# Moving the operands of TensorE's products to chosen offsets modulo 256 bytes in a four-layer decoder trunk

## Chip, cores and metric

One core of a Trainium2 chip. The metric is the device time of one execution in microseconds; lower is better.

## What is computed

The reference is a trunk of four residual layers over 256 tokens of width 1024, in float32: `x = x + mixer(rms_norm(x))`. Layers 0 and 3 use mixer A, layer 1 mixer B, layer 2 mixer C. Each mixer has one input projection, which also emits a gate z, and one output projection.

```python
def mixer_a(h):     # layers 0 and 3
    u, v, z = split(h @ w_in)                 # 3 x 2048 columns
    v = rms_norm(v, v_gain)
    mixed = einsum("gij,bcjgd->bcigd", tril(w_s), v) + b_s
    return (u * mixed * silu(z)) @ w_out
def mixer_b(h):     # layer 1
    q, k, v, z = split(h @ w_in)              # 3 groups x 8 heads x 128, z 1024
    o = softmax-weighted sum over 3 dilated window attentions of normed, rotated q, k
    return (o * silu(z)) @ w_out
def mixer_c(h):     # layer 2
    xc, z = split(h @ w_in)                   # 2 x 2048 columns
    mixed = per-group w_grp @ (causal_mean(xc, window) - xc) * scale
    return (mixed * silu(z)) @ w_out
```

## The kernel before

Every float32 matrix product is made of three products of a high and a low part (float32r). The helper `mm3` (L75) issues them: L77 multiplies the high stationary by the high moving operand, L78 the high stationary by the low moving one, L79 the low stationary by the high moving one. In `nc.tensor.matmul(out, a, b)` the operand `a` is stationary, 128 columns, and `b` is moving, 128, 256 or 512 columns. Each of these products has its own weight load, which the profile shows as PEld. In the names of the profile, `u<-w30h,hTh` is a product into the tile u whose moving operand is w30h and whose stationary one is hTh.

All weights come as one stream of 272 units of 512 KB, in the order of use. SP loads unit after unit into four buffers (wr). ACT makes the high part of a unit (L82) and DVE the low part (L85), into seven buffers each (w..h, w..l). `step` (L163) is called after every few products, runs due tasks (`tick`, L101) and splits units ahead of use. The order of all work on the engines is written out by these generators: a task issues some instructions and yields the number of ticks after which it goes on.

At the start of a layer `norm_task` and `norm_transpose` (L216 to L243) scale x, transpose it on TensorE (fp32, L222), and write the transposed, gained result as hTh (ACT, L226) and hTl (DVE, L229), each 8 x 256 columns. These two tiles, allocated once (L188, L189) and used by all layers, are read through `h_t` (128 columns, as the stationary operand) and `h_all` (256 columns, as the moving operand).

- `proj_tok` (L253): hT is stationary, 512 columns of w are moving. It makes v, z and u of layers 0 and 3, qk and v01 of layer 1, and the first gate (cz3) of layer 2. One call is 48 products. v2p (L708 to L715) is the same with 256 columns of w.
- `proj_feat` (L277): w is stationary, 256 columns of hT are moving. It makes bz of layer 1, and cx and the other cz of layer 2, 96 products in a call. `group` (L799) does the same with cd in place of hT, into cg, 48 products in a call.
- `proj_out` (L291): the gated result (y, yb or cy) is stationary, 512 columns of w are moving, into wo.
- In layer_a, `mix_task` (L401) multiplies wsr (stationary) by v (moving, 256 columns) into mx. In layer_b, `score_task` (L565) multiplies q (stationary) by k (moving, 128 or 256 columns) into s, and `product` (L641) the values v01 and v2 (stationary) by the transposed probabilities pT (moving, 128 or 256) into o.

SBUF tiles of a pool are laid end to end in the order in which their tags are first used, with all buffers of a tag together. Most sizes are whole multiples of 256 bytes. By these sizes w, the y tiles, v, wsr, qk, v01, pT, yb and cy begin 128 bytes past a multiple of 256, hT 64 bytes past one, and cd at a multiple.

The lines that the change touches are quoted here with the functions that hold them.

Of the kernel before, what the change touches and what calls it, by code (L numbers as in the profile page):

```python
# [48 lines left out]
def hybrid_trunk_kernel(ctx, tc, x, wts, norm_gainT, a_v_gain, a_wsT, a_bsT, b_gl, b_gv, c_scaleT,  # L49
# [18 lines left out]
    def tiny(n, name, tag="t"):  # L68
        return cp.tile([P, n], F32, tag=f"{tag}{n}", name=name, bufs=8)
# [115 lines left out]
    nc.gpsimd.memset(m05_row, -0.5)  # L185
    m05 = m05_row[:, :4]
    junk = cp.tile([P, HALF + 32], BF16, tag="junk", name="junk")[:, :HALF]
    hTh = cp.tile([P, KT, S], F32R, tag="hTh", name="hTh")  # L188
    hTl = cp.tile([P, KT, S], F32R, tag="hTl", name="hTl")  # L189

    warm = atp("warm")
    for _ in range(WARM):
# [23 lines left out]
    def norm_transpose(layer, t, xs):  # L216

        pts = []
        for n in range(2):
            pt = (trp if n else atp)(f"hp{layer}{t}{n}").rearrange("p (k c) -> p k c", c=P)  # L220
            for k in range(4):
                nc.tensor.transpose(pt[:, k], xs[:, n, k * P:(k + 1) * P], ident)  # L222
            pts.append(pt)
        sl = slice(t * P, (t + 1) * P)
        for k in range(KT):
            nc.scalar.activation(hTh[:, k, sl], pts[k // 4][:, k % 4], AF.Copy, scale=gT[:, layer, k:k + 1])  # L226
            yield k
        for k in range(KT):
            nc.vector.scalar_tensor_tensor(hTl[:, k, sl], pts[k // 4][:, k % 4], gT[:, layer, k:k + 1],  # L229
                                           hTh[:, k, sl].bitcast(F32), op0=ALU.mult, op1=ALU.subtract)  # L230
            yield KT + k
# [12 lines left out]

    def h_t(k, t):
        sl = slice(t * P, (t + 1) * P)
        return hTh[:, k, sl], hTl[:, k, sl]

    def h_all(k):
        return hTh[:, k, :], hTl[:, k, :]  # L250


    def proj_tok(name, skew=None):  # L253
# [94 lines left out]
        return kc, wsT, bsT  # L348

    def layer_a(layer, consts, pl, mid):  # L350
        kc, wsT, bsT = consts

        def tmp(tag, name, bufs):
# [6 lines left out]
        def v_task(n, o):  # L360
            vh, vl = pair(pl, [P, 2, HALF], "v", f"v{layer}{n}", 5)
            v.append((vh, vl))
            vv = [tmp("vv", f"vv{layer}{n}{t}", 2) for t in range(2)]
            for t in range(2):
                nc.scalar.activation(junk, o[t], AF.Square, accum_out=vs[t][:, n:n + 1])  # L365
                nc.vector.tensor_tensor(vv[t], o[t], kc[:, n * HALF:(n + 1) * HALF], op=ALU.mult)  # L366
            yield 1
            for t in range(2):
                hi_of(vh[:, t], vv[t])
            yield 1  # L370
            for t in range(2):
                lo_of(vl[:, t], vv[t], vh[:, t])
            done.add(("v", layer, n))
            if n < 3:
                return

            yield 1
            rs = []
            for t in range(2):
                ms = tiny(1, f"vms{layer}{t}")  # L380
                nc.vector.tensor_reduce(ms, vs[t], axis=mybir.AxisListType.X, op=ALU.add)
                me = tiny(1, f"vme{layer}{t}")
                nc.vector.tensor_scalar(me, ms, 1.0 / 2048.0, EPS, op0=ALU.mult, op1=ALU.add)
                r = tiny(1, f"vr{layer}{t}")
                nc.gpsimd.tensor_tensor(r, me, m05[:, 0:1], op=ALU.pow)
                rs.append(r)
            for t in range(2):
                yield 1
                wh, wl = pair(pl, [P, 8, P], "wsr", f"wsr{layer}{t}", 2)
                nc.scalar.activation(wh, wsT, AF.Copy, scale=rs[t][:, 0:1])  # L390
                yield 1
                nc.vector.scalar_tensor_tensor(wl, wsT, rs[t][:, 0:1], wh.bitcast(F32), op0=ALU.mult,
                                               op1=ALU.subtract)
                wsr.append((wh, wl))
            done.add(("wsr", layer))
            mid()
# [84 lines left out]
                                        cs[:, a, t:t + 1, :].to_broadcast([P, 2 * NG, ROPE]), op=ALU.mult)  # L481

    def layer_b(layer, consts, pl):
        gv, msk, rop = consts
        m0, m1 = msk[:, :NG * P], msk[:, NG * P:]
        yT = []
# [1 line left out]
        prob = {}  # L488

        def qk_task(hp, g, o):  # L490
            qh, ql = pair(pl, [P, 4, S], "qk", f"qk{hp}{g}", 4)
            qk[hp, g] = (qh, ql)
            ssq = [tiny(4, f"qs{hp}{g}{t}") for t in range(2)]
            rq = [tiny(4, f"qr{hp}{g}{t}") for t in range(2)]
            qn = [pl.tile([P, 4, HD], F32, tag="qn", name=f"qn{hp}{g}{t}", bufs=2) for t in range(2)]
# [15 lines left out]
            def rotate(t):  # L511

                ra = pl.tile([P, 4, ROPE], F32, tag="ra", name=f"ra{hp}{g}{t}", bufs=1)
                rb = pl.tile([P, 4, ROPE], F32, tag="rb", name=f"rb{hp}{g}{t}", bufs=1)
                for a in range(2):
                    hs = slice(2 * a, 2 * a + 2)
                    c = rop[:, 0, t, g, a:a + 1, :].to_broadcast([P, 2, ROPE])
                    nc.vector.tensor_tensor(ra[:, hs], qn[t][:, hs, :ROPE], c, op=ALU.mult)  # L518
                    for b in range(2):
                        s0, s1 = b * 16, (1 - b) * 16  # L520
                        c = rop[:, 1, t, g, a:a + 1, s0:s0 + 16].to_broadcast([P, 2, 16])
                        nc.vector.tensor_tensor(rb[:, hs, s0:s0 + 16], qn[t][:, hs, s1:s1 + 16], c, op=ALU.mult)  # L522
                nc.vector.tensor_tensor(qn[t][:, :, :ROPE], ra, rb, op=ALU.add)
# [3 lines left out]
            def transpose(t):  # L527
                pts[t] = trp(f"qt{hp}{g}{t}").rearrange("p (h c) -> p h c", c=P)
                for h in range(4):
                    nc.tensor.transpose(pts[t][:, h], qn[t][:, h], ident)  # L530
                for a in range(2):
                    nc.scalar.activation(qh[:, 2 * a:2 * a + 2, t * P:(t + 1) * P], pts[t][:, 2 * a:2 * a + 2],
                                         AF.Copy, scale=gv[:, 2 * g + a:2 * g + a + 1])

            def low(t):
                for a in range(2):
                    d = (slice(None), slice(2 * a, 2 * a + 2), slice(t * P, (t + 1) * P))
                    nc.vector.scalar_tensor_tensor(ql[d], pts[t][:, 2 * a:2 * a + 2], gv[:, 2 * g + a:2 * g + a + 1],  # L538
                                                   qh[d].bitcast(F32), op0=ALU.mult, op1=ALU.subtract)

            square(0)
            square(1)
# [22 lines left out]
        def score_task(hp, h):  # L565
# [8 lines left out]
            rl = [tiny(1, f"rl{hp}{h}{i}", "td") for i in range(2)]  # L574
            s0 = atp(f"s0{hp}{h}")
            for g in range(NG):
                qh, ql = qk[hp, g]
                mm3(s0[:, g * P:(g + 1) * P], (qh[:, h, :P], ql[:, h, :P]), (qh[:, 2 + h, :P], ql[:, 2 + h, :P]),
                    True, True)
            yield 1  # L580
            s1 = [atp(f"s1{hp}{h}{i}") for i in range(2)]
            for g in range(NG):
                qh, ql = qk[hp, g]
                mm3(s1[g // 2][:, (g % 2) * S:(g % 2 + 1) * S], (qh[:, h, P:], ql[:, h, P:]),
                    (qh[:, 2 + h], ql[:, 2 + h]), True, True)
            nc.vector.tensor_tensor_reduce(f0, s0[:, :NG * P], m0, 1.0, -3.0e38, op0=ALU.add, op1=ALU.max,
                                           accum_out=mx[0])
            nc.vector.tensor_scalar(nb[0], mx[0], -SCALE, None, op0=ALU.mult)
# [110 lines left out]
        for hp in range(NHEAD // 2):  # L699
            for g in range(NG):  # L700
                spawn(qk_task(hp, g, proj_tok(f"qk{hp}{g}", skew=layer if hp == 0 and g == 0 else None)))
                if hp == 0 and g == 0:
                    gate(0)
                    gate(1)
            o = proj_tok(f"v01{hp}")
            vh, vl = pair(pl, [P, 2, HALF], "v01", f"v01{hp}", 1)
            spawn(val_task(hp, o, vh, vl))
            vp = pp(f"v2p{hp}")  # L708
            for j in range(2):
                w = [a.rearrange("p a b -> p (a b)") for a in next_unit()]  # L710
                for kk in range(4):
                    k = 4 * j + kk
                    ws = [a[:, kk * 256:(kk + 1) * 256] for a in w]
                    for t in range(2):
                        mm3(vp[:, t * 256:(t + 1) * 256], h_t(k, t), ws, k == 0 and t == 0, k == KT - 1)  # L715
                    if kk % 2:
                        step(kk // 2)
            v2h, v2l = pair(pl, [P, 2, 256], "v2", f"v2{hp}", 1)
            spawn(val2_task(hp, vp, v2h, v2l))
            spawn(mix_task(hp, (vh, vl, v2h, v2l), szT[:, hp]), LAST_LAG if hp == NHEAD // 2 - 1 else MIX_LAG)  # L720

# [6 lines left out]


    def layer_c(layer, pl):  # L730
        csc = pl.tile([P, 32], F32, name="csc")[:, :16]
        nc.gpsimd.dma_start(csc, c_scaleT)
        rcn = pl.tile([P, 4, PAD], F32, name="rcn")
        nc.gpsimd.dma_start(rcn, rcnt)
# [34 lines left out]
        def pool_task(g, xp):  # L769
# [8 lines left out]
            for i in range(2):  # L778
                cur, lag = xc[i], 1
                while lag < w:  # L780
# [6 lines left out]
                d = pl.tile([P, 2, S], F32, tag="cdd", name=f"cdd{g}{i}", bufs=2)  # L787
                nc.vector.scalar_tensor_tensor(d, cur[:, :, PAD:], 1.0 / w, xc[i][:, :, PAD:], op0=ALU.mult,
                                               op1=ALU.subtract)
                e = pl.tile([P, 2, PAD], F32, tag="ce", name=f"ce{g}{i}", bufs=2)[:, :, :w - 1]  # L790
                nc.vector.tensor_tensor(e, cur[:, :, PAD:PAD + w - 1],
                                        rcn[:, g:g + 1, :w - 1].to_broadcast([P, 2, w - 1]), op=ALU.mult)
                nc.vector.tensor_tensor(d[:, :, :w - 1], e, xc[i][:, :, PAD:PAD + w - 1], op=ALU.subtract)
# [253 lines left out]
```

## Time and profile before

| what | value |
|---|---|
| time, median of 3 runs (lowest to highest) | 847.12 us (846.95 to 847.43) |
| the profiled execution's own time | 846.98 us |
| span of the profile, first to last instruction | 845.3 us |
| TensorE products: busy, count | 834.2 us, 4600 |
| TensorE weight loads: busy, count | 719.2 us, 4600 |
| DVE, ACT, POOL busy | 546.7, 488.6, 56.8 us |
| read from HBM | 147.72 MB |

The profile is of one execution. A product's duration there holds the filling of the array and overlaps with the next product, so the busy share of PE doesn't tell how dense the stream is. The start times do: the distance from the start of one product to the start of the next is what the product adds to the stream. The views of the trace give start times to 0.01 us, so the first and the last row of a stretch, with the number of products between, give the mean distance.

### The profile page before, as it was taken

The page shows a single profiled execution, that of the slowest core. Times are in us where ns is not written, and L with a number is a line of the kernel's source. Part 1 is how long each engine was busy: PE and PEld are TensorE (multiplying, and loading weights), DVE is VectorE, ACT ScalarE, POOL GpSimd, SP SyncE. Part 2 cuts the span into 40 slices and gives each one's busy share as a digit, 9 for nine tenths or more (in the row PEclk, how much of TensorE's full clock was granted, in tenths as well). Part 3 has the DMA queues.
Part 4 walks back from the last instruction along what each step waited for, and adds up shares of the span by engine and source line. Part 5 has one row for each costly group of instructions (what it writes and reads, how often), then busy time and mean ns, then how long its engine had stood idle before and what let it go on. Part 6 is the DMA issues. An engine that isn't in the chain of part 4 may idle for free.

```text
span 845.3 us, 12424 instructions
## 1 busy us (share of the span) xinstructions
PE 834.2 (99%) x4600; PEld 719.2 (85%) x4600; DVE 546.7 (65%) x932; ACT 488.6 (58%) x918; POOL 56.8 (7%) x79
## 2 busy tenths in 40 slices
PE   8999999999999999999999999999999999999998
PEld 6888888888988888888888889999988888888886
DVE  6866556546747667667667576798754786556551
ACT  7665444336768677678678567446543666434340
POOL 1301000001001021021021011000000000000000
PEclk9999999999999999999999999999999999999999
DMA  8756554562755345345345267547664476455541
GB/s 297 268 207 218 197 199 155 180 193 93 253 173 157 119 150 175 124 151 174 125 150 172 79 220 255 176 150 243 203 206 149 140 235 213 158 176 172 174 149 50
DMA packets 41500, 149.57 MB, mean 177 GB/s; under 512 B 4864, under 2 KB 4880, under 8 KB 41184
## 3 DMA queue, kind: packets, MB, share of 16 engines
q1 hardware_dynamic: 40320, 144.72, 51.9%
q0 software_dynamic: 976, 4.05, 1.5%
q8 instruction: 36, 0.59, 0.3%
q14 instruction: 24, 0.20, 0.1%
q10 hardware_dynamic: 144, 0.02, 0.0%
HBM read 147.72 MB, written 1.05 MB: 176 GB/s over the span
## 4 chain that ended last, share of the span: by engine, by line
PE 86%; ACT 7%; DVE 2%; issue 2%; POOL 2%; DMA 1%; SPq 0%; POOLq 0%; DVEq 0%
PE wo L77 6%; PE wo L78 6%; PE wo L79 6%; PE qk L79 4%; PE qk L77 4%; PE qk L78 4%; PE u L79 3%; PE z L79 3%; PE z L77 3%; PE u L77 3%; PE u L78 3%; PE z L78 3%; PE v L79 3%; PE v L77 3%; PE v L78 3%; ACT junk L500 2%
## 5 line engine op out<-in xcount | busy, mean ns | idle before, releaser
L505 POOL TENSOR_TENSOR qr<-qm,m 128x4 f32<-128x4 f32 x24 | 30.3, 1271 | 224.4 <-DVE qm L504 224.4
L509 ACT ACTIVATE qn<-qk,qr 128x128 f32<-128x128 f32 x96 | 27.5, 381 | 15.1 <-POOL qr L505 15.1
L500 ACT ACTIVATE junk<-qk 128x128 bf16<-128x128 f32 x96 | 26.8, 279 | 7.3 <-PE qk L79 4.6
L423 DVE TENSOR_TENSOR sz<-u,sz 128x512 f32<-128x512 f32 x16 | 11.0, 686 | 28.0 <-PE u L79 28.0
L226 ACT ACTIVATE hTh<-hp,gT 128x128 fp32r<-128x128 f32 x64 | 17.5, 382 | 16.1 <-PE hp L222 16.1
L207 POOL TENSOR_TENSOR r<-ms,m 128x1 f32<-128x1 f32 x8 | 5.4, 670 | 285.7 <-DVE ms L205 285.7
L321 DVE TENSOR_TENSOR x<-wo,x 128x512 f32<-128x512 f32 x16 | 11.0, 690 | 20.1 <-PE wo L79 20.0
L229 DVE SCALAR_TENSOR_TENSOR hTl<-hp,gT,hTh 128x128 fp32r<-128x128 f32 x64 | 17.9, 343 | 7.8 <-ACT hTh L226 7.8
L365 ACT ACTIVATE junk<-v 128x512 bf16<-128x512 f32 x16 | 9.6, 600 | 18.1 <-PE v L79 17.9
L500 ACT ACTIVATION_READ_ACCUMULATOR junk<-qk 128x1 f32 x96 | 19.1, 199 | 0.0
L366 DVE TENSOR_TENSOR vv<-v,kc 128x512 f32<-128x512 f32 x16 | 10.9, 689 | 12.7 <-ACT junk L365 12.6
L449 ACT ACTIVATE sz<-z 128x512 f32<-128x512 f32 x16 | 9.4, 597 | 15.5 <-PE z L79 14.9
L518 DVE TENSOR_TENSOR ra<-qn,kcb 128x64 f32<-128x64 f32 x48 | 10.6, 221 | 12.0 <-ACT qn L509 10.9
L530 PE MATMUL qt<-ident,qn 128*128 128x128 f32 x96 | 14.6, 274 | 3.4 <-DVE qk12l L538 0.5
L530 PEld LDWEIGHTS qt<-ident,qn 128*128 128x128 f32 x96 | 11.3, 140 | 7.3 <-issue 2.7
L200 ACT ACTIVATE junk<-x 128x512 bf16<-128x512 f32 x16 | 10.2, 639 | 10.9 <-DVE x L321 9.4
L426 DVE SCALAR_TENSOR_TENSOR yy<-mx,bs,sz 128x256 f32<-128x256 f32 x32 | 14.0, 480 | 0.6
L600 ACT ACTIVATE p<-p,rl 128x384 f32<-128x384 f32 (+1 forms) x16 | 11.5, 769 | 4.8 <-DVE rl L599 4.8
L522 DVE TENSOR_TENSOR rb<-qn,kcb 128x32 f32<-128x32 f32 x96 | 13.8, 184 | 0.0
L596 ACT ACTIVATE p<-p,nb 128x768 f32<-128x768 f32 x8 | 7.5, 938 | 7.9 <-DVE nb L595 7.9
L504 DVE TENSOR_SCALAR qm<-qs 128x4 f32<-128x4 f32 x24 | 3.3, 165 | 12.7 <-ACT junk L500 12.7
L346 POOL TENSOR_SCALAR_AFFINE_SELECT kc<-kc 128x128 f32<-128x128 f32 x16 | 9.2, 612 | 15.4 <-DMA kc<-in_a_wsT_dram 15.4
(2770 smaller groups left out, 3262.0 us busy)
## 6 DMA issues: line engine op xcount, KB each, us to landing
wr<-in_wts_dram SPq DMA_DIRECT2D x272, 512.0 KB, 4.2
kc<-in_a_v_gain_dram POOLq DMA_DIRECT2D x2, 1024.0 KB, 6.1
x<-in_x_dram SPq DMA_DIRECT2D x4, 256.0 KB, 4.9
kc<-in_a_wsT_dram POOLq DMA_DIRECT2D x2, 512.0 KB, 8.8
out_dram<-x SPq DMA_DIRECT2D x4, 256.0 KB, 2.0
kcb<-in_masks_dram POOLq DMA_DIRECT2D x1, 576.0 KB, 8.5
kcb<-in_b_gl_dram POOLq DMA_DIRECT2D x1, 192.0 KB, 6.0
kcb<-in_rope_dram POOLq DMA_DIRECT2D x1, 64.0 KB, 8.4
```

Of the source, the lines that this page charges most:

```text
L77: nc.tensor.matmul(out_ap, lh[0], rh[0], start=start, stop=False, skip_group_check=True)
L78: nc.tensor.matmul(out_ap, lh[0], rh[1], start=False, stop=False, skip_group_check=True)
L79: nc.tensor.matmul(out_ap, lh[1], rh[0], start=False, stop=stop, skip_group_check=True)
L226: nc.scalar.activation(hTh[:, k, sl], pts[k // 4][:, k % 4], AF.Copy, scale=gT[:, layer, k:k + 1])
L229: nc.vector.scalar_tensor_tensor(hTl[:, k, sl], pts[k // 4][:, k % 4], gT[:, layer, k:k + 1], hTh[:, k, sl].bitcast(F32), op0=ALU.mult, op ...
L426: nc.vector.scalar_tensor_tensor(y[:, sl], mxs[n][t][:, sl], bsT[:, 2 * n + gg:2 * n + gg + 1], us[t][:, sl], op0=ALU.add, op1=ALU.mult)
L500: nc.scalar.activation(junk[:, :HD], ov[t][:, h], AF.Square, accum_out=ssq[t][:, h:h + 1])
L505: nc.gpsimd.tensor_tensor(rq[t], ms, m05, op=ALU.pow)
L509: nc.scalar.activation(qn[t][:, h], ov[t][:, h], AF.Copy, scale=rq[t][:, h:h + 1])
L522: nc.vector.tensor_tensor(rb[:, hs, s0:s0 + 16], qn[t][:, hs, s1:s1 + 16], c, op=ALU.mult)
L530: nc.tensor.transpose(pts[t][:, h], qn[t][:, h], ident)
L600: nc.scalar.activation(f, f, AF.Copy, scale=rl[i][:, 0:1])
```

## The change

The change moves tiles in SBUF. hTh and hTl become slices of one tile hT with 64 spare elements; in layer 2 the slices begin at its start, in the other layers 16 elements (64 bytes) later. In layer A a tile st of 16 columns is allocated ahead of wsr, and holds the six small statistics that were in tiny tiles. In layer B the pair of tiles qk has 16 more columns and is split into a part for q, which begins 16 elements later than a multiple of 64, and a part for k, which begins at 0; rb is 16 columns longer; the low part of v2 is 48 columns longer. In layer C csc is 16 columns longer, and ce is 56 columns instead of 32. The number, the shapes and the order of the instructions stay.

```diff
-    hTh = cp.tile([P, KT, S], F32R, tag="hTh", name="hTh")
-    hTl = cp.tile([P, KT, S], F32R, tag="hTl", name="hTl")
+    hT = cp.tile([P, 2 * KT * S + 64], F32R, tag="hT", name="hT")
+
+    def h_parts(layer):
+
+        o = 0 if layer == 2 else 16
+        return [hT[:, o + i * KT * S:o + (i + 1) * KT * S].rearrange("p (k s) -> p k s", s=S) for i in range(2)]
+
+    hcur = [None, None]
...
         sl = slice(t * P, (t + 1) * P)
+        hTh, hTl = h_parts(layer)
         for k in range(KT):
...
     def h_t(k, t):
         sl = slice(t * P, (t + 1) * P)
-        return hTh[:, k, sl], hTl[:, k, sl]
+        return hcur[0][:, k, sl], hcur[1][:, k, sl]

     def h_all(k):
-        return hTh[:, k, :], hTl[:, k, :]
+        return hcur[0][:, k, :], hcur[1][:, k, :]
...
     def layer_a(layer, consts, pl, mid):
+        hcur[:] = h_parts(layer)
         kc, wsT, bsT = consts
...
             rs = []
-            for t in range(2):
-                ms = tiny(1, f"vms{layer}{t}")
+            st = pl.tile([P, 16], F32, name="st")
+            for t in range(2):
+                ms, me, r = (st[:, 8 * t + i:8 * t + i + 1] for i in range(3))
                 nc.vector.tensor_reduce(ms, vs[t], axis=mybir.AxisListType.X, op=ALU.add)
-                me = tiny(1, f"vme{layer}{t}")
                 nc.vector.tensor_scalar(me, ms, 1.0 / 2048.0, EPS, op0=ALU.mult, op1=ALU.add)
-                r = tiny(1, f"vr{layer}{t}")
                 nc.gpsimd.tensor_tensor(r, me, m05[:, 0:1], op=ALU.pow)
...
     def layer_b(layer, consts, pl):
+        hcur[:] = h_parts(layer)
...
         def qk_task(hp, g, o):
-            qh, ql = pair(pl, [P, 4, S], "qk", f"qk{hp}{g}", 4)
-            qk[hp, g] = (qh, ql)
+            parts = pair(pl, [P, 4 * S + 16], "qk", f"qk{hp}{g}", 4)
+
+            qk[hp, g] = [[a[:, o:o + 2 * S].rearrange("p (h s) -> p h s", s=S) for a in parts]
+                         for o in (2 * S + 16, 0)]
...
-                rb = pl.tile([P, 4, ROPE], F32, tag="rb", name=f"rb{hp}{g}{t}", bufs=1)
+                rb = pl.tile([P, 4 * ROPE + 16], F32, tag="rb", name=f"rb{hp}{g}{t}", bufs=1)
+                rb = rb[:, :4 * ROPE].rearrange("p (h c) -> p h c", c=ROPE)
...
             for g in range(NG):
-                qh, ql = qk[hp, g]
-                mm3(s0[:, g * P:(g + 1) * P], (qh[:, h, :P], ql[:, h, :P]), (qh[:, 2 + h, :P], ql[:, 2 + h, :P]),
-                    True, True)
+                qs, ks = qk[hp, g]
+                mm3(s0[:, g * P:(g + 1) * P], [a[:, h, :P] for a in qs], [a[:, h, :P] for a in ks], True, True)
...
-            v2h, v2l = pair(pl, [P, 2, 256], "v2", f"v2{hp}", 1)
+            v2h, v2l = [pl.tile([P, HALF + n], F32R, tag=f"v2{a}", name=f"v2{hp}{a}", bufs=1)[:, :HALF].rearrange(
+                "p (t c) -> p t c", t=2) for a, n in (("h", 0), ("l", 48))]
...
     def layer_c(layer, pl):
-        csc = pl.tile([P, 32], F32, name="csc")[:, :16]
+        hcur[:] = h_parts(layer)
+        csc = pl.tile([P, 48], F32, name="csc")[:, :16]
...
-                e = pl.tile([P, 2, PAD], F32, tag="ce", name=f"ce{g}{i}", bufs=2)[:, :, :w - 1]
+                e = pl.tile([P, 56], F32, tag="ce", name=f"ce{g}{i}", bufs=2)
+                e = e[:, :2 * PAD].rearrange("p (a s) -> p a s", s=PAD)[:, :, :w - 1]
```

## Rows read from the trace of the kernel before

**Rows 1.** The page, busy time of each engine (share of the span) and instructions

```profile
PE 834.2 (99%) x4600; PEld 719.2 (85%) x4600; DVE 546.7 (65%) x932; ACT 488.6 (58%) x918; POOL 56.8 (7%) x79
```

**Rows 2.** The page, TensorE's granted clock in 40 slices of the span, in tenths

```profile
PEclk9999999999999999999999999999999999999999
```

**Rows 3.** The page, the chain that ended last, by engine and by line

```profile
PE 86%; ACT 7%; DVE 2%; issue 2%; POOL 2%; DMA 1%; SPq 0%; POOLq 0%; DVEq 0%
PE wo L77 6%; PE wo L78 6%; PE wo L79 6%; PE qk L79 4%; PE qk L77 4%; PE qk L78 4%; PE u L79 3%; PE z L79 3%; PE z L77 3%; PE u L77 3%; PE u L78 3%; PE z L78 3%; PE v L79 3%; PE v L77 3%; PE v L78 3%; ACT junk L500 2%
```

**Rows 4.** Who waited for whom, TensorE: us in total, times, longest

```profile
PE qt L530 <- DVE qk12l L538: 0.5, 1, 0.5
```

**Rows 5.** Timeline of TensorE, z of layer 3: start us, us, instruction, count

```profile
700.20 0.39 PE L77 MATMUL z<-w224h,hTh 128*128 128x512 f32 x1
...
710.96 0.39 PE L79 MATMUL z<-w227h,hTl 128*128 128x512 f32 x1
```

**Rows 6.** Timeline of TensorE, wo of layer 3, second and last product

```profile
803.13 0.39 PE L78 MATMUL wo<-w258l,y30h 128*128 128x512 f32 x1
...
840.78 0.39 PE L79 MATMUL wo<-w271h,y33l 128*128 128x512 f32 x1
```

**Rows 7.** Timeline of TensorE, layer 1: a stretch of qk, one of wo

```profile
308.37 0.40 PE L78 MATMUL qk<-w98l,hTh 128*128 128x512 f32 x1
...
316.16 0.39 PE L79 MATMUL qk<-w101h,hTl 128*128 128x512 f32 x1
...
488.54 0.40 PE L78 MATMUL wo<-w149l,yb2h 128*128 128x512 f32 x1
...
496.29 0.39 PE L79 MATMUL wo<-w150h,yb3l 128*128 128x512 f32 x1
```

**Rows 8.** Timeline of TensorE, layer 2: one call into cz, one into cg

```profile
561.08 0.28 PE L77 MATMUL cz<-hTh,w174h 128*128 128x256 f32 x1
...
571.88 0.28 PE L79 MATMUL cz<-hTh,w177l 128*128 128x256 f32 x1
571.99 0.28 PE L77 MATMUL cg<-cd2h,w178h 128*128 128x256 f32 x1
...
577.58 0.28 PE L79 MATMUL cg<-cd2h,w179l 128*128 128x256 f32 x1
```

**Rows 9.** Timeline of TensorE: the 12 products of mx00, and 11 of v2p

```profile
72.69 0.28 PE L77 MATMUL mx<-v00h,wsr00h 128*128 128x256 f32 x1
...
73.99 0.28 PE L79 MATMUL mx<-v00h,wsr01l 128*128 128x256 f32 x1
...
267.00 0.28 PE L78 MATMUL v2p<-w88l,hTh 128*128 128x256 f32 x1
...
268.18 0.28 PE L79 MATMUL v2p<-w88h,hTl 128*128 128x256 f32 x1
```

**Rows 10.** Groups of TensorE, the fp32 transposes: busy us, mean ns, idle before

```profile
L434 PE MATMUL yp<-ident,yy 128*128 128x128 f32 x64 | 9.6, 272 | 0.0
L222 PE MATMUL hp<-ident,xs 128*128 128x128 f32 x64 | 8.5, 276 | 0.1
```

**Rows 11.** Instructions of tile wo, two units: duration ns min/median/max, first and last start

```profile
L77 PE MATMUL wo<-w49h,y00h x4: 393/397/476, 155.6 to 157.8; 128*128 128x512 f32 x4
L77 PE MATMUL wo<-w53h,y01h x4: 389/389/389, 167.1 to 169.1; 128*128 128x512 f32 x4
```

**Rows 12.** Timeline of TensorE, layer 1: bz from its second product after a transpose

```profile
219.89 0.28 PE L78 MATMUL bz<-hTl,w71h 128*128 128x256 f32 x1
...
222.48 0.28 PE L79 MATMUL bz<-hTh,w72l 128*128 128x256 f32 x1
```

**Rows 13.** Instructions of tile u, layer 0, one unit: duration ns min/median/max

```profile
L77 PE MATMUL u<-w20h,hTh x4: 394/394/394, 67.2 to 69.3; 128*128 128x512 f32 x4
L78 PE MATMUL u<-w20l,hTh x4: 388/388/388, 67.4 to 69.5; 128*128 128x512 f32 x4
L79 PE MATMUL u<-w20h,hTl x4: 392/392/392, 67.6 to 69.7; 128*128 128x512 f32 x4
```

More of the change, by code (lines that the diff above doesn't have):

```diff
@@ L531, in transpose @@
                 for a in range(2):
-                    nc.scalar.activation(qh[:, 2 * a:2 * a + 2, t * P:(t + 1) * P], pts[t][:, 2 * a:2 * a + 2],
-                                         AF.Copy, scale=gv[:, 2 * g + a:2 * g + a + 1])
+                    nc.scalar.activation(qk[hp, g][a][0][:, :, t * P:(t + 1) * P], pts[t][:, 2 * a:2 * a + 2], AF.Copy, scale=gv[:, 2 * g + a:2 * g + a + 1])
             def low(t):
                 for a in range(2):
-                    d = (slice(None), slice(2 * a, 2 * a + 2), slice(t * P, (t + 1) * P))
-                    nc.vector.scalar_tensor_tensor(ql[d], pts[t][:, 2 * a:2 * a + 2], gv[:, 2 * g + a:2 * g + a + 1],
-                                                   qh[d].bitcast(F32), op0=ALU.mult, op1=ALU.subtract)
+                    qh, ql = (b[:, :, t * P:(t + 1) * P] for b in qk[hp, g][a])
+                    nc.vector.scalar_tensor_tensor(ql, pts[t][:, 2 * a:2 * a + 2], gv[:, 2 * g + a:2 * g + a + 1],
+                                                   qh.bitcast(F32), op0=ALU.mult, op1=ALU.subtract)
             square(0)
@@ L582, in score_task @@
             for g in range(NG):
-                qh, ql = qk[hp, g]
-                mm3(s1[g // 2][:, (g % 2) * S:(g % 2 + 1) * S], (qh[:, h, P:], ql[:, h, P:]),
-                    (qh[:, 2 + h], ql[:, 2 + h]), True, True)
+                qs, ks = qk[hp, g]
+                mm3(s1[g // 2][:, (g % 2) * S:(g % 2 + 1) * S], [a[:, h, P:] for a in qs], [a[:, h] for a in ks],
+                    True, True)
             nc.vector.tensor_tensor_reduce(f0, s0[:, :NG * P], m0, 1.0, -3.0e38, op0=ALU.add, op1=ALU.max,
```

## The prediction

> **What bounds the kernel now.** I read the page's totals first. TensorE's matmul row is busy 834.2 of 845.3 us, while DVE has 546.7 and ACT 488.6 [rows 1]; the granted clock is at nine tenths or more in every slice [rows 2], that is at the 2.4 GHz level, so there is no clock to win. The chain that ended last is 86% PE, and its largest PE lines are the three products of the helper (L77, L78, L79) [rows 3]. The list of who waited for whom gives TensorE almost nothing: seven waits of 0.5 us at a transpose in layer 1, of which one row stands for all [rows 4], and little else. The kernel is a nearly unbroken stream of products, so its time is the sum of the distances between starts of neighbouring products. I therefore work with starts, not with durations, which include the filling of the array and overlap.
>
> Each product has a weight load of its own (the loads are busy 719.2 us beside the 834.2 of the products, so they overlap them [rows 1]), which reads the next stationary operand while the current moving one is still being read. I call "offset" the address of the next product's stationary operand minus that of the current moving one, modulo 256 bytes; it follows from the tile sizes laid end to end in order of first use. Before the change it is 192 for the projections from hT to 512 columns, and 0 for the output projections. With 256 columns it is 64 where w is stationary and hT moving (bz, cz, cx), 128 in cg, 0 in mx and, inside them, in s and o, and 192 in v2p. The kernel before is thus already an experiment on what the change does: the same helper with the same shapes at several offsets.
>
> - 512 columns, offset 192, layer 3: z from its first to its last product is 48 products, 47 distances, (710.96 - 700.20)/47 = 228.9 ns [rows 5].
> - 512 columns, offset 0, layer 3: wo from its second to its last is 166 distances, (840.78 - 803.13)/166 = 226.8 ns [rows 6]. Loops, operand shapes and PSUM use are the same as in z.
> - Layer 1, where other work cuts in: qk at offset 192 has 34 distances, (316.16 - 308.37)/34 = 229.1 ns; wo at offset 0 has 34, (496.29 - 488.54)/34 = 227.9 ns [rows 7].
> - 256 columns, offset 64: cz, 95 distances, (571.88 - 561.08)/95 = 113.7 ns; the same loop at offset 128 in cg, 47 distances, (577.58 - 571.99)/47 = 118.9 ns [rows 8].
> - 256 columns, offset 0: mx, 11 distances, (73.99 - 72.69)/11 = 118.2 ns; offset 192: v2p, 10 distances, (268.18 - 267.00)/10 = 118.0 ns [rows 9].
>
> The rows say that this offset has a price. cz and cg differ in nothing else that I can find: 5.2 ns of 119. These rows speak against a rule of the Trainium skill (TensorE: Matmul & The Clock Gate, "Step-by-step: what each phase is for"): TensorE has two independent read ports, and loading the next weights takes nothing from the running matmul. By that rule all the terms below are zero and the time stays at 847.12 us; that is rival B.
>
> **The change part by part.** No instruction is added or removed: operations, shapes, order and waits stay, only addresses move.
>
> - hT. The new tile is 256 bytes longer than the two it replaces, so everything behind it keeps its place modulo 256. In layers 0, 1 and 3 hT begins 64 bytes later and lies where w lies: offset 192 becomes 0. These are v, z and u of layers 0 and 3 (2 x 3 x 192 = 1152 products) and qk and v of layer 1 (576 + 192 = 768); without those whose successor is another kind, some 1126 and 724 are left. 1126 x (228.9 - 226.8) = 2.4 us, and 724 x (229.1 - 227.9) = 0.9 us: **-3.3 us**. Bounds: 1.2 ns for all 1850 is 2.2 us, 2.1 ns for all is 3.9 us. I keep the two prices apart because layer 1 is interrupted as its wo is. The 48 of layer 2's first cz stay at 192.
> - The side effect on hT as moving operand. bz in layer 1 goes from 64 to 0: 191 x (118.2 - 113.7) = **+0.9 us**. v2p goes from 192 to 0: 180 x (118.2 - 118.0), nothing. For both the nearest row at offset 0 is mx, another product, so bz is bounded by 0 and +1.0 (cg's price) and v2p by -0.8 (offset 64) and +0.2. In layer 2 the tile is taken 64 bytes earlier, so cx and cz stay at 64.
> - csc longer by 64 bytes: cd moves from 0 to 64, cg's offset from 128 to 64: 192 x (118.9 - 113.7) = **-1.0 us**; the longer ce brings cy back to w's place, so that layer's wo stays at 0.
> - st ahead of wsr (64 bytes): mx goes from 0 to 64. The padded rb does it for v01 and v2 (o), the split qk tile for s: q lies 64 past k, except where one group's last product meets the next group's tile. 88 + 68 + 50 products of 256 columns, some 204: 204 x (118.2 - 113.7) = **-0.9 us**. The 116 of 128 columns move the same way; no row shows them at 64. I take 0, since they read half as long, bounded by the 4.5 ns of 256 columns either way, 0.5 us.
> - The fp32 transposes of yy and p move from 0 to 64. They last 272 ns at 0 (yp) and 276 at 128 (hp) [rows 10]: 4 ns for each of 136 at most, half a microsecond, taken as 0.
> - The statistics in st instead of in turning tiny tiles, and hT's one tile for hi and lo: same instructions, same queues, no DMA moved past anything. The writers of hT are 64 pieces of 128 columns as before. Nothing is costed; their cover is the stream of products, and if it were gone an extra wait at a layer's start would cost like the 0.5 us waits [rows 4].
>
> What is late next: a shorter stream brings the transposes of layer 1 earlier to the same DVE work. Seven of them already wait [rows 4]. Between the two transposes of a task lie some 2.5 us of products; they shrink by under 1%, 0.02 us each, 7 x 0.02 = **+0.1 us**. DVE and ACT have 300 us of slack [rows 1].
>
> Sum: -3.3 + 0.9 - 1.0 - 0.9 + 0.1 = -4.2 us. The profiled execution takes 846.98 us (span 845.3), the median of the runs is 847.12, 0.14 more. 846.98 - 4.2 = 842.8, on the median's scale **842.9 us**.
>
> **The rivals.**
>
> A. The forecast: the offset sets the distance, 842.9. For it: cz against cg, z against wo, in the same helper [rows 5, 6, 8].
>
> B. The offset is no cause at 512 columns, or at none. Then 226.8 belongs to something else in wo, and what is left is -1.0 - 0.9 + 0.9 + 0.1 = -0.9, 846.2 us; if it is no cause at all, 847.1. For it: the 512-column difference is under 1% and the two sides are different stages; against it: it is there in layer 3 and again in layer 1 [rows 5 to 7], and the addresses are the only difference that I find. Here belongs also that the tiles don't land where I place them: with hT off by 64 bytes the 512-column term is gone and the time is again about 846.2.
>
> C. Slower: the offset helps only in an undisturbed stream. Some wo products at offset 0 last 397 ns instead of 389 [rows 11], and bz at offset 64 runs at (222.48 - 219.89)/22 = 117.7 ns for 22 distances after it was cut by a transpose, while it had 113.7 before [rows 12]. So there is a second, slower rhythm that the offset alone doesn't exclude. In that rhythm an offset-0 product costs 226.8 + 8 = 234.8, 5.9 more than now. It decides from the point where 2.1/8 = 26% of the 1850 fall into it; at 60% the mean is 231.6, 1850 x 2.7 = +5.0 us; with -0.9 for the rest this gives 851.2 us. Against it: layer 3's wo, 226.8, includes such products already, and layer 1's wo, the most interrupted one, still has 227.9 [rows 6, 7].
>
> **How the numbers follow.** A measurement of this kernel tells 0.2% (1.7 us) from no change. A has 0.86; its own ends are the bounds above: 3.9 + 1.0 + 0.9 with bz free and the unpriced half microseconds in favour, 6.3 us, 840.8; and 2.2 with the unpriced ones against it, about 1.5 to 2 us in all, 845.3. B has 0.10, C 0.04. The range reaches from 840.9 to 845.6: practically all of A, but not B and C (0.14 left out). Faster by over 0.2% is A less 0.01 for its weakest end: 0.85. Within 0.2% are B and that end: 0.11. Slower is C: 0.04.
>
> **What would show it.** In the profile after: z, u, v and qk at about 227 ns from start to start, their durations near 389 ns where they now go round 394, 388, 392 [rows 13]; cg and mx at 113 to 114 ns; bz at 118 or so; wo, cx and later cz as before; the waits of [rows 4] unchanged to 0.1 us. A z that stays at 228.9 makes it B; long stretches of 397 ns make it C. If bz stays at 113.7, only the step on bz is wrong, and the time is 0.9 us lower.

## The result, and the profile after

The change makes the kernel slower: 848.36 us median of 20 runs (847.85 to 848.80) against 846.99 us of 20 runs of the kernel before (846.27 to 847.65). The ratio is 1.0017 with a 95% interval of 1.001 to 1.0024. I had forecast 842.9 us, 4.2 us less; it is 1.4 us more.

The page of the kernel after shows the same picture as [rows 1] to [rows 3]: the same counts, the clock at nine tenths or more, 1 us more of PE.

```profile
span 846.6 us, 12421 instructions
PE 835.2 (99%) x4600; PEld 723.3 (85%) x4600; DVE 546.8 (65%) x932; ACT 488.8 (58%) x918; POOL 57.6 (7%) x79
PE 86%; ACT 7%; DVE 2%; issue 2%; POOL 2%; DMA 1%; SPq 0%; POOLq 0%; DVEq 0%
```

So the answer lies in the distances from start to start. Here is TensorE's timeline of the kernel after (start us, us, instruction, count), first and last row of each stretch, in this order: z and wo of layer 3, bz and v2p of layer 1, cz, cg and cx of layer 2.

```profile
702.29 0.39 PE L77 MATMUL z<-w224h,hT 128*128 128x512 f32 x1
...
712.95 0.39 PE L79 MATMUL z<-w227h,hT 128*128 128x512 f32 x1
...
804.47 0.39 PE L78 MATMUL wo<-w258l,y30h 128*128 128x512 f32 x1
...
842.12 0.39 PE L79 MATMUL wo<-w271h,y33l 128*128 128x512 f32 x1
...
208.78 0.28 PE L77 MATMUL bz<-hT,w68h 128*128 128x256 f32 x1
...
218.73 0.28 PE L79 MATMUL bz<-hT,w71l 128*128 128x256 f32 x1
...
266.89 0.28 PE L78 MATMUL v2p<-w88l,hT 128*128 128x256 f32 x1
...
268.09 0.28 PE L79 MATMUL v2p<-w88h,hT 128*128 128x256 f32 x1
...
562.53 0.28 PE L77 MATMUL cz<-hT,w174h 128*128 128x256 f32 x1
...
573.72 0.28 PE L79 MATMUL cz<-hT,w177l 128*128 128x256 f32 x1
...
573.84 0.28 PE L77 MATMUL cg<-cd2h,w178h 128*128 128x256 f32 x1
...
579.37 0.28 PE L79 MATMUL cg<-cd2h,w179l 128*128 128x256 f32 x1
...
522.96 0.28 PE L77 MATMUL cx<-hT,w160h 128*128 128x256 f32 x1
...
556.76 0.28 PE L79 MATMUL cx<-hT,w171l 128*128 128x256 f32 x1
```

z has 47 distances in 10.66 us, 226.8 ns where it had 228.9 [rows 5]; wo is unchanged, 37.65/166 = 226.8 [rows 6]. bz is now at 9.95/83 = 119.9 ns. The same stretch before, first and last row, had 9.43/83 = 113.6:

```profile
209.78 0.28 PE L77 MATMUL bz<-hTh,w68h 128*128 128x256 f32 x1
...
219.21 0.28 PE L79 MATMUL bz<-hTh,w71l 128*128 128x256 f32 x1
```

v2p is at 1.20/10 = 120 where it had 118.0 [rows 9]. cg came down only to 5.53/47 = 117.7 from 118.9. And cz, whose offset the change leaves at 64, is at 11.19/95 = 117.8 ns where it had 113.7 [rows 8]; the 288 products of cx go the same way, 33.80/287 = 117.8. The view of one tile's instructions (duration ns min/median/max, first and last start) shows it for cx at a glance, first before, then after:

```profile
L77 PE MATMUL cx<-hTh,w160h x8: 276/276/276, 522.7 to 525.1; 128*128 128x256 f32 x8
```

```profile
L77 PE MATMUL cx<-hT,w160h x8: 281/282/282, 523.0 to 525.4; 128*128 128x256 f32 x8
```

The distances of these products, summed by kind over both traces and subtracted, give where the time went. A row can change by up to 0.2 us with the way in which the distances at the seams between kinds are counted:

| products | offset | forecast us | measured us |
|---|---|---|---|
| z, u, v of layers 0, 3 | 192 to 0 | -2.4 | -1.96 |
| qk, v of layer 1 | 192 to 0 | -0.9 | -0.52 |
| bz | 64 to 0 | +0.9 | +1.09 |
| v2p | 192 to 0 | 0 | +0.30 |
| cg | 128 to 64 | -1.0 | -0.19 |
| mx, s, o of 256 columns | 0 to 64 | -0.9 | -0.06 |
| cx | 64, kept | 0 | +1.67 |
| cz of 256 columns | 64, kept | 0 | +1.06 |
| sum | | -4.3 | +1.39 |

All starts of TensorE together, from the first to the last, span 1.34 us more than before, so the kinds that the table leaves out add up to almost nothing; the medians differ by 848.36 - 846.99 = 1.37. The open question was thus why products at an unchanged offset became some 4.4 ns slower. TensorE's timeline at the second pair of transposes of layer 2's first gate gives the hint: before it, cz settles at 113 to 114 ns in both kernels. This is the last transpose and what follows, before:

```profile
515.82 0.27 PE L757 MATMUL czt<-ident,czs 128*128 128x128 f32 x1
515.84 0.37 PE L77 MATMUL cz<-hTh,w157h 128*128 128x256 f32 x1
516.05 0.28 PE L78 MATMUL cz<-hTl,w157h 128*128 128x256 f32 x1
516.17 0.28 PE L79 MATMUL cz<-hTh,w157l 128*128 128x256 f32 x1
516.28 0.28 PE L77 MATMUL cz<-hTh,w157h 128*128 128x256 f32 x1
...
517.19 0.28 PE L79 MATMUL cz<-hTh,w157l 128*128 128x256 f32 x1
```

and after:

```profile
515.78 0.27 PE L768 MATMUL czt<-ident,czs 128*128 128x128 f32 x1
515.81 0.36 PE L77 MATMUL cz<-hT,w157h 128*128 128x256 f32 x1
516.01 0.28 PE L78 MATMUL cz<-hT,w157h 128*128 128x256 f32 x1
516.12 0.28 PE L79 MATMUL cz<-hT,w157l 128*128 128x256 f32 x1
516.24 0.28 PE L77 MATMUL cz<-hT,w157h 128*128 128x256 f32 x1
...
517.18 0.28 PE L79 MATMUL cz<-hT,w157l 128*128 128x256 f32 x1
```

From the fourth product behind the transpose to the last one shown are 8 distances: 0.91 us, 113.8 ns, before; 0.94 us, 117.5 ns, after. Both streams then hold their pace, before to the first cg and after to the last. The products are the same ones at the same offset; something ahead of them decides between two paces.

### The profile page after: what moved, and what is told of

Same layout as the page of the kernel before. It is cut to its first block, busy times and chain, and to the rows that moved or that the text cites. A ratio compares the mean times of both kernels' runs of the same rounds, so it can differ in the third digit from the quotient of the medians.

```text
span 846.6 us, 12421 instructions
## 1 busy us (share of the span) xinstructions
PE 835.2 (99%) x4600; PEld 723.3 (85%) x4600; DVE 546.8 (65%) x932; ACT 488.8 (58%) x918; POOL 57.6 (7%) x79
## 4 chain that ended last, share of the span: by engine, by line
PE 86%; ACT 7%; DVE 2%; issue 2%; POOL 2%; DMA 1%; SPq 0%; POOLq 0%; DVEq 0%
PE wo L77 6%; PE wo L79 6%; PE wo L78 6%; PE qk L77 4%; PE qk L79 4%; PE qk L78 4%; PE z L77 3%; PE z L79 3%; PE u L77 3%; PE u L78 3%; PE z L78 3%; PE u L79 3%; PE v L78 3%; PE v L79 3%; PE v L77 3%; ACT junk L510 2%
## 5 line engine op out<-in xcount | busy, mean ns | idle before, releaser
L233 ACT ACTIVATE hT<-hp,gT 128x128 fp32r<-128x128 f32 x64 | 17.5, 382 | 16.0 <-PE hp L228 16.0
L236 DVE SCALAR_TENSOR_TENSOR hT<-hp,gT,hT 128x128 fp32r<-128x128 f32 x64 | 17.9, 343 | 7.7 <-ACT hT L233 7.7
```

## The experiments

Two theories stood first. M: the offset counts modulo 512 bytes, and the 256 bytes that hT grew by (so that w moved by 256 against hT) turned a good 64 into a bad 320. R: at offset 64 the stream has two rhythms, that is two steady distances from start to start, 113.5 and 118 ns; each holds itself, and what goes before decides which is entered.

**e1_pad512.** hT grows by 512 bytes instead of 256.

```diff
-    hT = cp.tile([P, 2 * KT * S + 64], F32R, tag="hT", name="hT")
+    hT = cp.tile([P, 2 * KT * S + 128], F32R, tag="hT", name="hT")
```

> The changed kernel with 128 spare elements in hT instead of 64, so that all tiles behind hT stand where they stood modulo 512 bytes, not only modulo 256. Theory M (the offset counts modulo 512: 64 is good for 256 columns, 64 + 256 is not): cx and the last three cz of layer 2 go from 118 back to 113.5 ns from start to start, 2.7 us less, about 845.7 us. Theory R (offset 64 allows two rhythms, 113.5 and 118 ns, each of which holds itself; what goes before decides which one is entered): nothing before layer 2's first transposes changes in time, so cx and cz stay at 118 and the time at about 848.4 us. In both, z, u, v and qk stay at 227 ns and bz at 120.

848.37 us (8 runs, ratio 1.0014, 1.0003 to 1.0025); cx at 117.8, bz at 119.9, z at 226.7 ns. M predicted 845.7: it is wrong.

**e4b_w256** puts the same question from the other side: the kernel before, with all of w moved by 256 bytes against hT. (An earlier try of the same kernel, e4_w256, has two runs, 2980.16 and 847.72 us. Its profile is of the long one, in which a cx product takes 410 ns from start to start, and no pace is read from it.)

```diff
-    hTh = cp.tile([P, KT, S], F32R, tag="hTh", name="hTh")
-    hTl = cp.tile([P, KT, S], F32R, tag="hTl", name="hTl")
+    hT = cp.tile([P, 2 * KT * S + 64], F32R, tag="hT", name="hT")
+    hTh, hTl = [hT[:, i * KT * S:(i + 1) * KT * S].rearrange("p (k s) -> p k s", s=S) for i in range(2)]
```

> The kernel before with hTh and hTl as halves of one tile that is 256 bytes longer, once more: a run on record of it was disturbed from its first to its last product. Theory M (offsets count modulo 512): 850.7 us, bz, cx and cz at 118. Theory P: bz, cx and cz as before, 847.0 us.

847.16 us (8 runs), ratio 1.000 (0.999 to 1.001); bz at 113.7 and cx at 113.3 ns as before. Modulo 512 doesn't matter here, and one tile for both halves of hT costs nothing.

**e2_cg128.** cg back at its old offset.

```diff
-        csc = pl.tile([P, 48], F32, name="csc")[:, :16]
+        csc = pl.tile([P, 32], F32, name="csc")[:, :16]
...
-                e = pl.tile([P, 56], F32, tag="ce", name=f"ce{g}{i}", bufs=2)
+                e = pl.tile([P, 2 * PAD], F32, tag="ce", name=f"ce{g}{i}", bufs=2)
```

> The changed kernel with csc and ce of the kernel before, so that cg's offset is 128 again instead of 64; hT, w and the cx and cz products stay where the change puts them. Theory R: the stretch from the second pair of transposes of layer 2 to the first cg stays at 118 ns (its 60 cz and 288 cx products), cg goes to 119, and what follows a cg is thrown into the fast rhythm, as before the change: the 96 cz, 96 cx and 96 cz after the cgs go from 118 to 113.7, 288 x 4.2 = 1.2 us less, cg 0.2 us more: about 847.4 us. Theory M: all cx and cz stay at 118; about 848.5 us.

845.85 us (8 runs, ratio 0.9984, 0.9972 to 0.9995), 2.5 us under the changed kernel. Both theories missed: cx is fast from its start, ahead of any cg. The timeline, first and last cx ahead of the first cg:

```profile
522.76 0.28 PE L77 MATMUL cx<-hT,w160h 128*128 128x256 f32 x1
...
555.29 0.28 PE L79 MATMUL cx<-hT,w171l 128*128 128x256 f32 x1
```

32.53/287 = 113.3 ns. So cg isn't what set cx's pace. But the edit of csc moved all tiles of layer 2 back by 64 bytes, among them czs, the stationary operand of the gate's transposes. That is where theory R was mended into theory P: the transposes leave TensorE in one of the two rhythms, and where czs lies decides in which.

**e3_late.** The same transposes one step later, all addresses kept.

```diff
                 nc.scalar.activation(sz[t], zp[t], AF.Silu)
-            yield 2
+            yield 3
```

> The changed kernel with every address kept, but the transposes of layer 2's first gate one step (6 products) later. Theory M, and any theory in which addresses alone set the distance: cx and cz stay at 118 ns, 848.4 us within 0.3. Theory R: the stream comes out of the transposes at another phase, so cx may enter the fast rhythm (113.5 ns, up to 2.7 us less, 845.7 us) or stay in the slow one; if it comes out fast, addresses alone are refuted, if it stays slow, nothing is decided.

848.18 us (8 runs), cx at 117.8 ns: slow as before the edit, nothing decided. It does say that this shift by one step doesn't undo the slow entry.

**e5_czs0.** The changed kernel; czs goes back, and with it the two tiles ahead of it (rcn and the gate's transposed tile sz). What ACT and DVE write from cd on stays moved.

```diff
-        csc = pl.tile([P, 48], F32, name="csc")[:, :16]
+        csc = pl.tile([P, 32], F32, name="csc")[:, :16]
...
             sz = [tmp("czs", f"czs{g}{t}", 2) for t in range(2)]
+            pl.tile([P, 16], F32, name="padb")
```

> The changed kernel with csc as before and an unused 64 bytes behind czs: the gate's tiles czs, which the transposes of layer 2 read as stationary operand, stand at 0 modulo 256 again instead of 64, while cd, xc, nx, cdd and cy stay where the change puts them and cg keeps offset 64. Theory P (the transposes leave TensorE in one of two rhythms, and where czs lies decides in which; the offset-64 products then keep it): cz and cx at 113.5 ns again, 2.7 us less, and cg, entered in the fast rhythm at offset 64, at 113.5 instead of 117.8, 0.8 us less: 844.8 us. Theory X (the 64 bytes by which the tiles that ACT and DVE write in layer 2 moved make those engines disturb the products): cd, xc, nx and cy are still moved, so cz, cx and cg stay at 118, about 848.4 us.

844.63 us (7 runs), ratio 0.997 (0.9959 to 0.9981). P's 844.8 is met and X's 848.4 is not. Timeline of cx and cg:

```profile
522.89 0.28 PE L77 MATMUL cx<-hT,w160h 128*128 128x256 f32 x1
...
555.41 0.28 PE L79 MATMUL cx<-hT,w171l 128*128 128x256 f32 x1
...
571.85 0.28 PE L77 MATMUL cg<-cd2h,w178h 128*128 128x256 f32 x1
...
577.17 0.28 PE L79 MATMUL cg<-cd2h,w179l 128*128 128x256 f32 x1
```

cx 32.52/287 = 113.3 ns, and cg 5.32/47 = 113.2 ns: the same cg, at the same offset of 64, has 117.7 in the changed kernel. In both it goes at the pace of the products ahead of it.

**e8_czs64.** The converse, in the kernel before: of all tiles, modulo 256 bytes, only czs moves.

```diff
+            pl.tile([P, 16], F32, name="pada")
             sz = [tmp("czs", f"czs{g}{t}", 2) for t in range(2)]
+            pl.tile([P, 48], F32, name="padb")
```

> The kernel before with 64 unused bytes ahead of czs and 192 behind it, so that of all tiles modulo 256 bytes only czs moves, from 0 to 64. No product of 256 or 512 columns has another offset than before. Theory P: the second pair of transposes leaves the slow rhythm, cz and cx of layer 2 run at 118 until the first cg; cg at its old offset of 128 ends that rhythm (before, cz and cx came out of cg at 113.7), so 60 cz and 288 cx products are slower by 4.5 ns, 1.6 us more: 848.6 us. Theory X and any theory of the products' own offsets: nothing changes, 847.0 us.

848.82 us (10 runs), ratio 1.002 (1.001 to 1.0029), where P said 848.6. Timeline of cx, ahead of the first cg, and of the cz behind it:

```profile
523.85 0.28 PE L77 MATMUL cx<-hTh,w160h 128*128 128x256 f32 x1
...
557.65 0.28 PE L79 MATMUL cx<-hTh,w171l 128*128 128x256 f32 x1
...
563.47 0.28 PE L77 MATMUL cz<-hTh,w174h 128*128 128x256 f32 x1
...
574.24 0.28 PE L79 MATMUL cz<-hTh,w177l 128*128 128x256 f32 x1
```

33.80/287 = 117.8 ns, then 10.77/95 = 113.4 ns. One tile that none of these products reads makes 348 of them slower, until the 48 products of cg at offset 128 end the slow rhythm. The changed kernel took that end away too: its cg at 64 passes the slow rhythm on, and all of layer 2's later 256-column products keep it. Besides the transposes, only ACT touches czs, when it writes it:

```profile
L752 ACT ACTIVATE czs<-cz x2: 598/598/598, 511.0 to 512.0; 128x512 f32<-128x512 f32 x2
```

That is over at 512.6 us, and the cz products between the two pairs of transposes still settle at 113 to 114 ns; the slow stretch begins behind the second pair, at 516.7. So the pace changes at the second pair, 4 us after ACT's write. Over all profiles but the long one it comes out the same way: with czs at 64 (changed kernel, e1, e3, e6, e8) cx runs at 117.8 ns, with czs at 0 (kernel before, e2, e4b, e5, e7, e9) at 113.3.

**e6_layer1.** The changed kernel with hT at its old place in layer 1.

```diff
-        o = 0 if layer == 2 else 16
+        o = 0 if layer in (1, 2) else 16
```

> The changed kernel with hT at its old place in layer 1 too (as it has it in layer 2). Offsets there as before: bz 64, v2p 192, qk and v 192. By the two traces: bz -1.1 us, v2p -0.3, qk and v +0.5 us: 847.5 us. If the 512-column gain of layer 1 is as large as I predicted (0.9 us) and bz and v2p cost only 0.9, the time stays at 848.4. cx and cz at 118 unless layer 2 is entered otherwise.

847.32 us (10 runs), 1.0 us under the changed kernel: bz and v2p cost more there than qk and v gain. The timeline of bz:

```profile
208.86 0.28 PE L77 MATMUL bz<-hT,w68h 128*128 128x256 f32 x1
...
218.28 0.28 PE L79 MATMUL bz<-hT,w71l 128*128 128x256 f32 x1
```

9.42/83 = 113.5 ns against 119.9.

**e9_hT_A.** The 512-column term alone: the kernel before with hT 64 bytes later in layers 0 and 3, and nothing else.

```diff
-    hTh = cp.tile([P, KT, S], F32R, tag="hTh", name="hTh")
-    hTl = cp.tile([P, KT, S], F32R, tag="hTl", name="hTl")
+    hT = cp.tile([P, 2 * KT * S + 64], F32R, tag="hT", name="hT")
...
+        o = 16 if layer in (0, 3) else 0
...
```

The lines left out hand the slices of hT to the layers, as in the change itself.

> The kernel before with one edit: hT stands 64 bytes later in layers 0 and 3 and as before in layers 1 and 2; st, qk, rb, v2, csc, ce as before. It prices the 512-column term by itself: z, u and v of the two layers at 227.2 ns instead of 229, 1120 products x 1.75 = 2.0 us less, 845.1 us. By my predicted price of 2.1 ns it is 844.7. A theory in which the offset at 512 columns is no cause says 847.0.

845.18 us (10 runs), ratio 0.9975 (0.9966 to 0.9984), 2.2 us under the 847.37 of the kernel before in that series. The timeline of z in layer 3:

```profile
699.00 0.39 PE L77 MATMUL z<-w224h,hT 128*128 128x512 f32 x1
...
709.66 0.39 PE L79 MATMUL z<-w227h,hT 128*128 128x512 f32 x1
```

10.66/47 = 226.8 ns; in the kernel before 228.9, with no other difference than hT's address (that it is one tile costs nothing, e4b). The mx products of layers 0 and 3, whose two operands stay where they were, changed too: their eight runs of 12 have a mean distance of 119.4 ns where they had 118.0. What changed for them is the pace of the 512-column products ahead.

**e7_both.** The repairs of e5 and e6 together.

> The two repairs together: czs at 0 modulo 256 and hT at its old place in layer 1. If they add, 844.6 - 1.0 = 843.6 us, that is 3.5 us under the kernel before: z, u and v of layers 0 and 3 at 227 ns, cz, cx and cg at 113.5, bz at 113.5 or so, qk and v of layer 1 at 229. If layer 2 is entered at another phase because layer 1 is timed otherwise, cz, cx and cg go back to 118 and the time to about 847.3 us.

843.47 us (5 runs), ratio 0.9956 (0.9942 to 0.997): they add, and this version beats both kernels, by 3.9 us the one before and by 4.9 the changed one. cx is again at 32.52/287 = 113.3 ns:

```profile
span 841.1 us, 12421 instructions
520.89 0.28 PE L77 MATMUL cx<-hT,w160h 128*128 128x256 f32 x1
...
553.41 0.28 PE L79 MATMUL cx<-hT,w171l 128*128 128x256 f32 x1
```

## Why the prediction was wrong

**The step that failed** is the reading of [rows 8] and [rows 9] as prices of an offset: 113.7 ns at 64, 118.9 at 128, 118.2 at 0. 113.7 is not the price of offset 64 but of one of two rhythms that a stream at offset 64 can be in; the other costs 117.8. Offset 64 permits the fast rhythm and does not bring it. From this follow three of the terms that missed:

- "In layer 2 the tile is taken 64 bytes earlier, so cx and cz stay at 64" was right of the address and wrong of the time: I put these products at nothing, and they cost +2.7 us. e8, which moves czs alone, and e5 show that this hangs on czs. The prediction doesn't name that tile: the longer csc moves it by 64 bytes with the rest of layer 2, and of the transposes I priced only those of yy and p, at 4 ns each. The price of moving czs was not in its transposes but in the 636 products of cx and cz behind them.
- cg, forecast -1.0, got -0.19, since it was entered in the slow rhythm; entered in the fast one (e5) it has 113.2 ns, as the forecast of 113 to 114 has it.
- mx, s and o, forecast -0.9, got -0.06. mx, at 64 now, has 117.8 ns in all eight runs, the slow pace of cx. That it was entered slow is one reading, since it comes in runs of 12 behind products of 512 columns; no run tried to enter it fast. Another reading follows below.

I had the counter-example in my hands: [rows 12] show bz at offset 64 at 117.7 ns for a whole stretch after a transpose. I used it for rival C, on the 512-column products, and not on the 672 products of cx and cz for which I relied on 113.7.

**What isn't shown: that the difference of the two addresses is what counts.** Wherever a run has 113 ns, the moving tile (hT or cd) lies at 64 modulo 256 and the stationary one is w. In mx the change made the difference 64 by moving the stationary tile instead, and 113 ns did not come. The moving tile's own address would explain the 256-column rows of 113 ns as well as the difference does. It is not the whole either: in v2p only the stationary tile moved, and its stretch went from 118.0 to 120.0. No run holds the difference and moves both tiles.

**The 512-column term** was right in mechanism as far as the address goes. z went to 226.8 as forecast, and e9 shows that hT's address alone is a cause there, so rival B is out. The size was off: -2.5 instead of -3.3 us. In layers 0 and 3, 1.96 us over some 1126 products is 1.7 ns for each instead of 2.1; in layer 1, 0.52/724 = 0.7 instead of 1.2. The trace shows where the rest is. In layer 1, of the distances between qk and v products, those from the second to the eleventh behind an interruption (342) have a mean of 229.9 ns before and 230.2 after; only the 324 later ones came down, from 228.9 to 226.7. So in layer 1 the gain was full in an undisturbed stream and nothing just behind an interruption. That is the first half of rival C. Its second half, that an interrupted product becomes dearer than it was, did not show.

This is also where the trace bears on the rule of the Trainium skill (TensorE: Matmul & The Clock Gate, "Step-by-step: what each phase is for") that loading the next weights takes nothing from the running matmul. With the shapes, the order and the engines' other work the same, 64 bytes of address changed the distance by 2.1 ns in z (e9), and by 6.4 ns in bz (e6 against the changed kernel). So the pace of a stream of loads and products depends here on where its operands lie; whether the two reads hinder one another, or one of them is slower at some addresses by itself, these runs don't separate.

**bz** was forecast at +0.9 and measured at +1.09: the sign was right, and its first stretch rose by 6.3 ns where I took mx's 4.5. **v2p** was to cost nothing, within -0.8 and +0.2; it cost 0.30. Both used mx's 118.2 ns for offset 0, and those 12 products are too few to have settled. The later part of the stretch of [rows 9] reads, before:

```profile
73.39 0.28 PE L77 MATMUL mx<-v00h,wsr01h 128*128 128x256 f32 x1
...
73.99 0.28 PE L79 MATMUL mx<-v00h,wsr01l 128*128 128x256 f32 x1
```

0.60/5 = 120 ns, which is what bz (119.9) and v2p (120) now have. (The 88, 68 and 50 products of mx, s and o add up to 206, not 204; that changes nothing in the term.)

**What is late next** (+0.1 us) was right as far as it can be seen: the waits of [rows 4] stand at 0.5 to 0.6 us in the kernel after.

**The chances.** The cases were built on whether the offset matters; the case that came true, the offset matters and a stream's history matters as much, was not among them. The measured ratio of 1.0017 lies in the band that I called no change, which had 0.11. So 0.85 for "faster" was too high, with rows on the table that showed one offset at two paces.

## What to carry to other kernels

When one kind of instruction shows two paces under the same conditions in one trace, explain the two before pricing anything with either: a mean over a stretch is then a property of the stretch, not of the condition that it is filed under. In a stream of products that TensorE never leaves, look at what stands just ahead of a stretch whose pace changed (a transpose, another shape), not only at the stretch itself, and read its starts one by one across the seam. And move one tile at a time: e8 names a tile that no slow product reads.

## What the runs showed that I had not expected

- Products of 256 columns, each with a load of its own, at offset 64: 113.2 to 113.8 ns or 117.5 to 117.8 ns from start to start, each held for as long as the stream runs (cx: 287 distances at 113.3 in e5, at 117.8 in e8). Offset 128 (cg) had 118.7 to 118.9 in every run that has it, offset 0 in long streams (bz) 119.9.
- A stream in the slow rhythm that passes through 48 products at offset 128 comes out fast (e8: 117.8 ahead of cg, 113.4 behind it). One that passes through 48 at offset 64 comes out as it went in (changed kernel: 117.8 ahead and behind; e5: 113.3).
- The seam after the second pair of transposes: where czs lay at 0 the first distance was some 206 ns and the stream was fast (before, e5); where it lay at 64 the first distance was some 201 ns and the stream slow (after, e8). The first pair of the changed kernel also had 201 ns and yet reached the fast pace after five products, so this number alone doesn't decide.
- Nor does the address of the transposed tile alone. Behind the first transposes that cut bz, e6 has hT at 64 as the kernel before has it, and qn, which they read, lies alike modulo 256 by the tile sizes (other tiles of layer 1 lie as in the changed kernel); the first distance is 201 ns in both. Yet the stretch of [rows 12] stays at 117.7 ns, and in e6 the same stretch turns fast after five products: (221.47 - 218.95)/22 = 114.5. What in the chip sets the two paces, and what a transpose changes in it, stays open.

```profile
218.95 0.28 PE L78 MATMUL bz<-hT,w71h 128*128 128x256 f32 x1
...
221.47 0.28 PE L79 MATMUL bz<-hT,w72l 128*128 128x256 f32 x1
```
